# Dividing softmax rows on GpSimd: a per-row scalar operand in place of a repeated column

## The chip, the cores and the metric

The kernel runs on one core of one Trainium2 chip. A core has a matrix engine (TensorE, PE in the profile, with its weight loads as PEld), a vector engine (VectorE, DVE), an activation engine (ScalarE, ACT), a general engine (GpSimd, POOL) and a queue engine (SyncE, SP) that issues most transfers. The metric is device time in microseconds (us). Before the change three runs gave 652.29, 652.94 and 653.63 us, a median of 652.94.

## The reference, cut to what matters

The model is a two-layer encoder trunk over 512 tokens of width 1024, all in fp32. Layer 0 mixes tokens by neighbourhood attention with 16 heads of width 64 (each query sees an 8 x 16 window of a 64-wide grid), layer 1 by dense latent attention with 16 heads (query and key width 96, value width 64). Around both stand RMS norms, a SiLU gate, an output projection and a gated per-layer embedding. What the change touches is the softmax of both attentions:

```python
# layer 0, per grid row of queries
s = jnp.einsum('bwhd,biwjhd->bhwij', q_r, k_win).astype(jnp.float32) * scale
s = (s + bias[None]).reshape(B, H, GRID_W, kr * kc)
pr = jax.nn.softmax(s, axis=-1).reshape(B, H, GRID_W, kr, kc).astype(v.dtype)
return jnp.einsum('bhwij,biwjhd->bwhd', pr, v_win)
...
# layer 1, per block of 128 queries
s = jnp.einsum('bqhd,bkhd->bhqk', qblk, k).astype(jnp.float32) * scale
pr = jax.nn.softmax(s, axis=-1).astype(v.dtype)
return jnp.einsum('bhqk,bkhd->bqhd', pr, v)
```

The softmax is exp(s - max) divided by its sum over the keys; queries lie on partitions, so the sum is one number per partition.

## The kernel before, in words

Matrix products of fp32 data are made of three products each: every operand is split into a high part (`hi`) and a rest (`lo`), and high x high, high x rest and rest x high are added up in PSUM. For weights the split is an ACT copy (L100) and a subtraction that runs mostly on POOL (L101); for activations it is `split` (L109 to L114), an ACT copy from PSUM (L110) and a DVE subtraction (L112).

**Neighbourhood attention** is `na_heads` (L406), with eight pairs of heads, and `na_head` (L536) for one head. A head is worked in two halves of two query tiles. For a half, PE writes scores to a bank `ps_S` (L558, L559); DVE adds the bias and takes the row maximum, writing to the tile `ex` (L565, L568); ACT makes the exponentials in place and their row sums `sm` (L576); DVE takes reciprocals `rc` (L578); POOL multiplies each query tile of `ex` by its column of `rc` (L582, 128 x 128 for the first query tile and 128 x 256 for the other three). Then PE transposes `ex` block by block (L594, L596) into banks `ps_T`, ACT and DVE split these into `ph` and `pl`, and PE multiplies with the values into `ps_O` (L608). The tile `ex` has two buffers: DVE can write the scores of a head only once the transposes of the head two before it are done. The projections of the next pair (L123, `ps_mm`), the gate `z` and the output projection are PE's other work there.

**Latent attention** is `mla_heads` (L942) with 64 turns of `score` (L1041), one for each head and block of 128 queries: three matmuls into `ps_S`, a row maximum on DVE (L1052), exponentials and sums on ACT (L1054), a reciprocal on DVE (L1055), and POOL's multiplication of the whole 128 x 512 tile (L1056). `turn` (L1058) transposes the tile three turns later (L155) and splits it; `output` (L1066) multiplies with the values (L1071). `ex` has four buffers here. Pieces of projection for the next heads are laid between by a table (`pieces`, L1082).

**What sets the order.** Each engine runs its instructions in the order in which they stand in its queue. In most of the program a scheduler lays that order down when the kernel is built: it plays the program through with durations that it assumes for each operation, and puts an instruction where, by these, its operands are there. Where the code says `issue_after`, an instruction stands behind a named one. In latent attention the loop at L1152 ties PE's work, turn by turn, to the last matmul before it, so PE's order is mostly the code's there; in neighbourhood attention it is the scheduler's.

Of the kernel before, what the change touches and what calls it, by code (L numbers as in the profile page):

```python
# [16 lines left out]
ALU = mybir.AluOpType  # L17
AX = mybir.AxisListType
PSUM = bass.MemoryType.PSUM
P = 128  # L20
S = 512
# [13 lines left out]
def win(t, r0, r1, off, dims):  # L35

    b = t[r0:r1]
    return bass.AP(tensor=b.tensor, offset=b.offset + off, ap=[list(b.ap[0])] + [list(d) for d in dims])
# [18 lines left out]
class Trunk:  # L57
# [478 lines left out]
    def na_head(self, pool, h, sq, s0, dk, kl, vh):  # L536

        nc = self.nc
        bias = pool.tile([P, 384], F32, name="bias", tag="bias", bufs=3)
        self.last_bias = nc.sync.dma_start(bias, self.a["na_bias"][h])  # L540
        ex = pool.tile([P, 896], F32, name="ex", tag="ex", bufs=2)
        mx = self.small.tile([P, 4], F32, name="mx", tag="mx")
        sm = self.small.tile([P, 4], F32, name="sm", tag="sm")
        rc = self.small.tile([P, 4], F32, name="rc", tag="rc")
        ecol = lambda qt: slice(0, 128) if qt == 0 else slice(256 * qt - 128, 256 * qt + 128)
        for half in range(2):
            sp = self.psum("S")
            for i in range(2):
                qt = 2 * half + i
                o = sp[:, i * 256:(i + 1) * 256]  # L550
                if qt == 0:
                    o = o.rearrange("p (a b) -> p a b", a=2)
                    lq = s0
                    K = lambda t: win(t, 0, P, 0, [[384, 2], [1, P]])
                else:
                    lq = sq[:, qt * P - 64:qt * P + 64]
                    K = lambda t: t[:, (qt - 1) * P:(qt + 1) * P]
                nc.tensor.matmul(o, lq, K(dk), start=True, stop=False)  # L558
                nc.tensor.matmul(o, lq, K(kl), start=False, stop=True)  # L559
            for i in range(2):  # L560
                qt = 2 * half + i
                c = slice(qt, qt + 1)
                if qt == 0:
                    for r, sc in ((slice(0, 64), slice(0, 128)), (slice(64, 128), slice(128, 256))):
                        nc.vector.tensor_tensor_reduce(out=ex[r, 0:P], in0=sp[r, sc], in1=bias[r, 0:P], scale=-1.0,  # L565
                                                       scalar=-NEG, op0=ALU.add, op1=ALU.min, accum_out=mx[r, c])
                else:
                    nc.vector.tensor_tensor_reduce(out=ex[:, ecol(qt)], in0=sp[:, i * 256:(i + 1) * 256],  # L568
                                                   in1=bias[:, P:], scale=-1.0, scalar=-NEG, op0=ALU.add, op1=ALU.min,
                                                   accum_out=mx[:, c])  # L570
            hs = slice(2 * half, 2 * half + 2)
            for i in range(2):
                qt = 2 * half + i
                e = ex[:, ecol(qt)]
                with self.tc.issue_after(self.hold):
                    self.last_exp = nc.scalar.activation(e, e, AF.Exp, scale=-1.0, bias=mx[:, qt:qt + 1],  # L576
                                                         accum_out=sm[:, qt:qt + 1])
            nc.vector.reciprocal(rc[:, hs], sm[:, hs])  # L578
            for i in range(2):
                qt = 2 * half + i  # L580
                e = ex[:, ecol(qt)]
                self.last_norm = nc.gpsimd.tensor_tensor(out=e, in0=e, in1=rc[:, qt:qt + 1].to_broadcast([P, e.shape[1]]),  # L582
                                                         op=ALU.mult)


        pts = []
        E = lambda qt, s: ex[:, 256 * qt - 128 + s * P:256 * qt + s * P]
        apart = lambda t, w, d: win(t, 0, P, 0, [[d, 2], [1, w]])
        for blocks in ([(None, ex[:, 0:P]), (64, E(1, 0)), (320, E(3, 1))],
                       [(0, E(1, 1)), (128, E(2, 0)), (256, E(2, 1)), (384, E(3, 0))]):  # L590
            t = self.psum("T")
            for c, b in blocks:
                if c is None:
                    nc.tensor.transpose(apart(t, 64, 448), b, self.ident)  # L594
                else:
                    nc.tensor.transpose(t[:, c:c + P], b, self.ident)  # L596
            ph = pool.tile([P, S], F32R, name="ph", tag="pt", bufs=8)
            pl = pool.tile([P, S], F32R, name="pl", tag="pt", bufs=8)
            if len(blocks) == 3:
                self.split(apart(ph, 192, 320), apart(pl, 192, 320), apart(t, 192, 320))  # L600
            else:
                self.split(ph, pl, t)
            pts.append((ph, pl))
        O = self.psum("O")
        n = 0
        for kt, o, w, g, c in ((0, 0, 192, 0, 0), (3, 320, 192, 0, 320), (1, 64, 256, 1, 0), (2, 192, 256, 1, 256)):
            for s in pts[g]:
                nc.tensor.matmul(O[:, o:o + w], vh[kt], s[:, c:c + w], start=n == 0, stop=n == 7,  # L608
                                 skip_group_check=True)
                n += 1  # L610
        return O
# [330 lines left out]
    def mla_heads(self, pool, xT, cT, sets, oT):  # L942


        nc, a = self.nc, self.a
# [95 lines left out]
        def score(i):  # L1041
            h, qt = i // 4, i % 4
            st = sets[h // 2 % 2]
            q, k, kk = ((st["qe"], st["ke"], 96), (st["qo"], st["ko"], 128))[h % 2]
            if qt == 0:
                ST[h] = [self.small.tile([P, 4], F32, name=n, tag=n) for n in ("mx", "sm", "rc")]
            mx, sm, rc = (t[:, qt:qt + 1] for t in ST[h])
            sp = self.psum("S")
            Q = lambda s: q[s][0:kk, qt * P:(qt + 1) * P]
            K = lambda s: k[s][0:kk, :]  # L1050
            self.mms(sp, [(Q(0), K(0)), (Q(0), K(1)), (Q(1), K(0))])
            nc.vector.reduce_max(mx, sp, axis=AX.X, negate=True)  # L1052
            ex = EX[i] = pool.tile([P, S], F32, name="ex", tag="ex", bufs=4)
            nc.scalar.activation(ex, sp, AF.Exp, bias=mx, accum_out=sm)  # L1054
            nc.vector.reciprocal(rc, sm)  # L1055
            nc.gpsimd.tensor_tensor(out=ex, in0=ex, in1=rc.to_broadcast([P, S]), op=ALU.mult)  # L1056

        def turn(i):  # L1058
            h, qt = i // 4, i % 4
# [92 lines left out]
        for i in range(70):  # L1152
            work = []
            if i < 64:
                work.append(lambda: score(i))
                work += pieces(i // 8)[i % 8]
            elif i < 68:
                work.append(ple)
            if 3 <= i < 67:
                work.append(lambda: turn(i - 3))  # L1160
            if i >= 8 and i % 4 < 2:
                work.append(lambda: output(i // 4 - 2, i % 4))
            for f in work:
                with self.tc.issue_after(self.last_mm.ins):
                    f()
            if i == 53:
                last = self.last_mm
# [307 lines left out]
```

## Time and profile before

The profiled execution took 653.56 us; its span, from the first to the last instruction, is 651.5 us, so 2.06 us lie around the span. The execution lies 0.62 us above the median of the three runs.

| | busy, us | share of the span |
|---|---|---|
| PE | 640.2 | 98% |
| PEld | 541.9 | 83% |
| ACT | 453.4 | 70% |
| DVE | 427.7 | 66% |
| POOL | 408.4 | 63% |

The neighbourhood attention runs from about 105 to 235 us, the latent attention from about 400 to 556 us. The mean granted PE clock is 0.995 of full speed. PE's matmuls overlap at their ends, so a row's duration is longer than the step from one matmul to the next; the step is read from the starts. An idle time in brackets behind a row is that of the engine just before it, with the work that ended it.

### The profile page before, as it was taken

How to read it: one execution, taken by the hardware profiler on the slowest of the kernel's cores; microseconds unless marked ns; L12 is line 12 of the kernel's file. 1: busy time of each engine (PE TensorE's matmuls, PEld its weight loads, DVE VectorE, ACT ScalarE, POOL GpSimd, SP SyncE). 2: the span in 40 equal slices, each digit the busy share in tenths (PEclk: the TensorE clock that was granted, in tenths of full speed). 3: DMA queues.
4: the chain of work that ended last, by engine and by line, in shares of the span. 5: the costliest groups of instructions: out<-in, count | busy, mean ns of one | idle time of the engine just before them, and what ended most of it. 6: DMA issues, size and time to landing. Idle time of an engine off the chain costs nothing.

```text
span 651.5 us, 9980 instructions
## 1 busy us (share of the span) xinstructions
PE 640.2 (98%) x3299; PEld 541.9 (83%) x3299; DVE 427.7 (66%) x886; ACT 453.4 (70%) x903; POOL 408.4 (63%) x371
## 2 busy tenths in 40 slices
PE   9999999999999999999999999999999999999994
PEld 6888878888888888888999887888888888888884
DVE  6197987565665616569715514898988885474665
ACT  7575766887886733788644535897989897547855
POOL 0471006877978853797655516786969887437974
PEclk9999999999999999999999999999999999999997
DMA  9939725778958989446643245120112223683524
GB/s 326 355 124 306 217 66 179 263 205 217 229 209 217 239 178 342 147 154 188 224 140 102 78 109 156 32 75 24 49 50 66 65 84 112 229 292 126 193 65 162
DMA packets 46131, 107.41 MB, mean 165 GB/s; under 512 B 4736, under 2 KB 17792, under 8 KB 46080
## 3 DMA queue, kind: packets, MB, share of 16 engines
q1 hardware_dynamic: 34608, 87.12, 39.3%
q0 software_dynamic: 11040, 18.88, 13.6%
q10 hardware_dynamic: 432, 0.79, 0.3%
q8 instruction: 26, 0.43, 0.3%
q14 instruction: 25, 0.20, 0.1%
HBM read 95.23 MB, written 25.17 MB: 185 GB/s over the span
## 4 chain that ended last, share of the span: by engine, by line
PE 83%; POOL 1%; ACT 1%; DVE 0%; DMA 0%; issue 0%; POOLq 0%
PE ps_mm L123 27%; PE ps_S L123 10%; PE ps_mm L959 7%; PE ps_T L155 6%; PE ps_T L851 5%; PE ps_O L1071 5%; PE ps_mm L851 3%; PE ps_S L851 3%; PE ps_O L608 2%; PE ps_T L123 2%; PE ps_O L123 2%; PE ps_mm L909 2%; PE ps_T L301 2%; PE ps_T L596 2%; PE ps_S L909 1%; PE ps_S L559 1%
## 5 line engine op out<-in xcount | busy, mean ns | idle before, releaser
L101 POOL TENSOR_TENSOR wwlo<-wraw,wwhi 128x1024 fp32r<-128x1024 f32 (+5 forms) x68 | 122.3, 1810 | 93.5 <-ACT wwhi L100 41.9
L796 POOL TENSOR_TENSOR wlo<-wraw,whi 128x512 fp32r<-128x512 f32 x56 | 72.7, 1331 | 22.3 <-ACT whi L794 20.2
L1056 POOL TENSOR_TENSOR ex<-ex,rc 128x512 f32<-128x512 f32 x64 | 66.2, 1043 | 26.6 <-DVE rc L1055 22.5
L100 ACT ACTIVATE wwhi<-wraw 128x1024 fp32r<-128x1024 f32 (+5 forms) x71 | 55.1, 799 | 34.3 <-PE ps_mm L123 18.9
L1054 ACT ACTIVATE ex<-ps_S,mx 128x512 f32<-128x512 f32 x64 | 44.0, 687 | 12.6 <-DVE mx L1052 10.9
L1052 DVE TENSOR_REDUCE mx<-ps_S 128x1 f32<-128x512 f32 x64 | 43.7, 683 | 8.4 <-PE ps_S L123 7.7
L582 POOL TENSOR_TENSOR ex<-ex,rc 128x128 f32<-128x128 f32 (+1 forms) x64 | 37.5, 701 | 17.7 <-DVE rc L578 17.5
L112 DVE TENSOR_TENSOR pt_lo<-ps_T,pt_hi 128x512 fp32r<-128x512 f32 x64 | 43.1, 680 | 7.1 <-ACT pt_hi L110 6.7
L110 ACT ACTIVATE pt_hi<-ps_T 128x512 fp32r<-128x512 f32 x64 | 37.7, 594 | 3.4 <-PE ps_T L155 3.0
L155 PE MATMUL ps_T<-ident,ex 128*128 128x128 f32 x256 | 38.3, 272 | 0.0
L155 PEld LDWEIGHTS ps_T<-ident,ex 128*128 128x128 f32 x256 | 31.5, 140 | 7.5
L123 PE MATMUL ps_mm<-xh,wwhi 128*128 128x512 f32 x120 | 33.7, 404 | 0.0
L221 DVE TENSOR_TENSOR u<-ps_O,u 64x512 f32<-64x512 f32 x32 | 21.9, 685 | 17.7 <-ACT u L220 17.2
L576 ACT ACTIVATE ex<-ex,mx 128x128 f32<-128x128 f32 (+1 forms) x64 | 30.2, 473 | 4.2 <-DVE mx L565 4.1
L123 PE MATMUL ps_mm<-xl,wwhi 128*128 128x512 f32 x120 | 31.9, 395 | 0.0
L794 ACT ACTIVATE whi<-wraw 128x1024 fp32r<-128x1024 f32 x28 | 29.3, 1057 | 3.2 <-DMA wraw<-sum 2.4
L123 PE MATMUL ps_mm<-xh,wwlo 128*128 128x512 f32 x120 | 31.1, 394 | 0.0
L123 PE MATMUL ps_S<-ke,qe 96*128 96x512 f32 x96 | 28.9, 407 | 0.3 <-DMA qe<-rl 0.3
L123 PE MATMUL ps_S<-ko,qo 128*128 128x512 f32 x96 | 28.9, 409 | 0.0
L959 PE MATMUL ps_mm<-cT,wwhi 128*128 128x512 f32 x94 | 27.7, 393 | 0.0
L220 ACT ACTIVATE u<-ps_O 64x512 f32<-64x512 f32 x32 | 18.9, 591 | 12.0 <-PE ps_O L608 8.8
L225 POOL TENSOR_TENSOR u<-u,z 128x512 f32<-128x512 f32 x16 | 22.6, 1412 | 7.5 <-DVE u L221 7.5
(488 smaller groups left out, 1915.1 us busy)
## 6 DMA issues: line engine op xcount, KB each, us to landing
sum<-gate POOLq DMA_DIRECT2D x12, 1024.0 KB, 8.2
wraw<-na_qk SPq DMA_DIRECT2D x16, 512.0 KB, 4.9
wraw<-sum SPq DMA_DIRECT2D x16, 512.0 KB, 3.3
pe<-pe SPq DMA_DIRECT2D x31, 256.0 KB, 5.9
wraw<-gate SPq DMA_DIRECT2D x12, 512.0 KB, 3.3
wraw<-na_v SPq DMA_DIRECT2D x10, 512.0 KB, 3.4
sum<-sum POOLq DMA_DIRECT2D x4, 1024.0 KB, 11.1
wraw<-na_o SPq DMA_DIRECT2D x8, 512.0 KB, 4.8
```

Of the source, the lines that this page charges most:

```text
L100: nc.scalar.activation(hi[:, c], raw[:, c], AF.Copy)
L101: f = lambda e, c=c: e.tensor_tensor(out=lo[:, c], in0=raw[:, c], in1=hi[:, c].bitcast(F32), op=ALU.subtract)
L110: self.last_copy = self.act.activation(hi, src, AF.Copy, scale=scale)
L112: self.dve.tensor_tensor(out=lo, in0=src, in1=hi.bitcast(F32), op=ALU.subtract)
L123: last = self.last_mm = nc.tensor.matmul(out, l, r, start=i == 0, stop=i == n - 1)
L155: self.last_mm = self.nc.tensor.transpose(t[:, i * P:(i + 1) * P], b, self.ident)
L796: nc.gpsimd.tensor_tensor(out=lo[:, o], in0=raw[:, o], in1=hi[:, o].bitcast(F32), op=ALU.subtract)
L851: mm = nc.tensor.matmul(ps, l, r, start=j == 0 and p in banks, stop=j == 11 and p in (2, 3, 4), skip_group_check=True)
L959: self.last_mm = nc.tensor.matmul(PS[key], *terms[i], start=i == 0, stop=i == len(terms) - 1)
L1052: nc.vector.reduce_max(mx, sp, axis=AX.X, negate=True)
L1054: nc.scalar.activation(ex, sp, AF.Exp, bias=mx, accum_out=sm)
L1056: nc.gpsimd.tensor_tensor(out=ex, in0=ex, in1=rc.to_broadcast([P, S]), op=ALU.mult)
```

## The change

Both divisions keep their place in the program, their engine, their data and their result. Instead of a tensor-by-tensor multiplication, whose second tensor is the column `rc` read again for each element of a row, they become a tensor-by-scalar multiplication, whose scalar is one number per partition, read from the same column. There are 64 of them in neighbourhood attention (16 of 128 x 128 and 48 of 128 x 256) and 64 of 128 x 512 in latent attention.

```diff
@@ na_head
             for i in range(2):
                 qt = 2 * half + i
                 e = ex[:, ecol(qt)]
-                self.last_norm = nc.gpsimd.tensor_tensor(out=e, in0=e, in1=rc[:, qt:qt + 1].to_broadcast([P, e.shape[1]]),
-                                                         op=ALU.mult)
+                self.last_norm = nc.gpsimd.tensor_scalar(e, e, rc[:, qt:qt + 1], None, op0=ALU.mult)
@@ score
             nc.vector.reciprocal(rc, sm)
-            nc.gpsimd.tensor_tensor(out=ex, in0=ex, in1=rc.to_broadcast([P, S]), op=ALU.mult)
+            nc.gpsimd.tensor_scalar(ex, ex, rc, None, op0=ALU.mult)
```

The scheduler takes the new operation into account, and the order changes on all engines from the neighbourhood attention on. The changed kernel is a line shorter, so its lines behind L582 are numbered one lower (L594 becomes L593, L1056 becomes L1055).

**PE, in the middle of neighbourhood attention.** `ps_T_1504` and `ps_T_1512` hold the transposes of head 5 (counted from 0), `ps_O_1463` is the output of head 4, `ps_S_1625` holds scores of head 6 and `ps_S_1683` of head 7. Before:

```order
L594 MATMUL ps_T_1504<-ident_71,ex_1475 128x2x64
L608 MATMUL ps_O_1463<-ph_1450,Q00_679 128x192
L558 MATMUL ps_S_1625<-da_1403,s0_1411 128x256
L608 MATMUL ps_O_1463<-pl_1451,Q00_679 128x192
L608 MATMUL ps_O_1463<-ph_1450,Q10_502 128x192
L608 MATMUL ps_O_1463<-pl_1451,Q10_502 128x192
L608 MATMUL ps_O_1463<-ph_1459,Q00_679 128x256
L608 MATMUL ps_O_1463<-pl_1460,Q00_679 128x256
L608 MATMUL ps_O_1463<-ph_1459,Q10_502 128x256
L608 MATMUL ps_O_1463<-pl_1460,Q10_502 128x256
L596 MATMUL ps_T_1504<-ident_71,ex_1475 128x128 x2
L596 MATMUL ps_T_1512<-ident_71,ex_1475 128x128 x4
```

And now:

```order
L593 MATMUL ps_T_1504<-ident_71,ex_1475 128x2x64
L558 MATMUL ps_S_1683<-db_1404,s0_1413 128x256
L595 MATMUL ps_T_1504<-ident_71,ex_1475 128x128
L595 MATMUL ps_T_1512<-ident_71,ex_1475 128x128
L559 MATMUL ps_S_1683<-lb1_513,s0_1413 128x256
L558 MATMUL ps_S_1683<-db_1404,sb_1367 128x256
L559 MATMUL ps_S_1683<-lb1_513,sb_1367 128x256
L558 MATMUL ps_S_1696<-db_1404,sb_1367 128x256
L595 MATMUL ps_T_1512<-ident_71,ex_1475 128x128 x2
```

The transposes of head 5 stood beside the scores of head 6 and now stand among those of head 7: a head's transposes have moved further behind its scores.

**PE, at the end of neighbourhood attention.** `ps_T_2259` and `ps_T_2267` hold the transposes of head 12, `ps_O_2276` is its output, `ps_mm_2509` a projection for the gate, `ps_S_2355` holds scores of head 14, `ps_S_2413` of head 15, `ps_T_2317` transposes of head 13. Before:

```order
L594 MATMUL ps_T_2259<-ident_71,ex_2230 128x2x64
L596 MATMUL ps_T_2259<-ident_71,ex_2230 128x128
L596 MATMUL ps_T_2267<-ident_71,ex_2230 128x128
L559 MATMUL ps_S_2305<-lb0_509,sb_1979 128x256
L596 MATMUL ps_T_2267<-ident_71,ex_2230 128x128 x2
L123 MATMUL ps_mm_2509<-xh0_158,wwhi_2504 128x512
L123 MATMUL ps_mm_2509<-xh1_159,wwhi_2504 128x512 x2
L596 MATMUL ps_T_2259<-ident_71,ex_2230 128x128
L596 MATMUL ps_T_2267<-ident_71,ex_2230 128x128
L123 MATMUL ps_mm_2509<-xh1_159,wwhi_2504 128x512 x2
L123 MATMUL ps_mm_2509<-xl0_160,wwhi_2504 128x512 x4
L558 MATMUL ps_S_2355<-da_2216,s0_2224 128x256
```

And now:

```order
L593 MATMUL ps_T_2259<-ident_71,ex_2230 128x2x64
L595 MATMUL ps_T_2259<-ident_71,ex_2230 128x128
L595 MATMUL ps_T_2267<-ident_71,ex_2230 128x128 x3
L595 MATMUL ps_T_2259<-ident_71,ex_2230 128x128
L595 MATMUL ps_T_2267<-ident_71,ex_2230 128x128
L607 MATMUL ps_O_2276<-ph_2263,Q01_680 128x192
L558 MATMUL ps_S_2413<-db_2217,s0_2226 128x256
L559 MATMUL ps_S_2413<-lb1_513,s0_2226 128x256
L558 MATMUL ps_S_2413<-db_2217,sb_2180 128x256
L559 MATMUL ps_S_2413<-lb1_513,sb_2180 128x256
L593 MATMUL ps_T_2317<-ident_71,ex_2288 128x2x64
```

The projection `ps_mm_2509`, which stood between the transposes and what needs them, has moved ahead of this place; the output of head 12 now follows its own transposes with one transpose between.

**POOL, in latent attention.** `wwlo` are weight rests, `rl` a rotary key or query part, `u` and `o1l` belong to the gated output. Before:

```order
L101 TENSOR_TENSOR wwlo<-wraw,wwhi 128x512 x2
L995 TENSOR_TENSOR rl<-rl,rope_s 128x512
L1056 TENSOR_TENSOR ex<-ex,rc 128x512
L996 TENSOR_TENSOR rl<-rh,rl 128x512
L1056 TENSOR_TENSOR ex<-ex,rc 128x512 x2
L998 TENSOR_TENSOR rl<-rl,rh 128x512
L101 TENSOR_TENSOR wwlo<-wraw,wwhi 128x192 x2
L1056 TENSOR_TENSOR ex<-ex,rc 128x512 x3
L225 TENSOR_TENSOR u<-u,z 128x512
```

And now:

```order
L101 TENSOR_TENSOR wwlo<-wraw,wwhi 128x512 x2
L994 TENSOR_TENSOR rl<-rl,rope_s 128x512
L1055 TENSOR_SCALAR ex<-ex,rc 128x512 x3
L995 TENSOR_TENSOR rl<-rh,rl 128x512
L1055 TENSOR_SCALAR ex<-ex,rc 128x512 x2
L997 TENSOR_TENSOR rl<-rl,rh 128x512
L101 TENSOR_TENSOR wwlo<-wraw,wwhi 128x192 x2
L225 TENSOR_TENSOR u<-u,z 128x512
L1055 TENSOR_SCALAR ex<-ex,rc 128x512 x3
```

Two divisions have moved ahead of the rotary sum; PE's order beside them is the same there.

## The prediction

> **What bounds the kernel now.** I read the shares of busy time first, then the chain that ended last, then what PE waited for.
>
> ```profile
> span 651.5 us, 9980 instructions
> PE 640.2 (98%) x3299; PEld 541.9 (83%) x3299; DVE 427.7 (66%) x886; ACT 453.4 (70%) x903; POOL 408.4 (63%) x371
> PE 83%; POOL 1%; ACT 1%; DVE 0%; DMA 0%; issue 0%; POOLq 0%
> PE ps_T L301 <- ACT s L51: 1.2, 1, 1.2
> PE ps_T L596 <- POOL ex L582: 0.3, 1, 0.3
> ```
>
> PE is busy for 98% of the span, the chain is PE's to 83% and POOL's to 1%, and in all PE waited for a division once, for 0.3 us. Ends of matmuls are modelled, so I looked whether their starts hide stalls:
>
> ```profile
> 148.44 1.98 PE L123 MATMUL ps_mm<-xl,wwhi 128*128 128x512 f32 x8
> 150.25 1.98 PE L123 MATMUL ps_mm<-xh,wwlo 128*128 128x512 f32 x8
> 152.07 0.27 PE L594 MATMUL ps_T<-ident,ex 128*128 128x128 f32 x1
> ```
>
> Eight matmuls of 512 columns take 1.81 and 1.82 us from start to start, 0.227 us each; PE keeps that step through both attentions. POOL's place in the two stages that the change touches is read from stretches within them and from POOL's groups there:
>
> ```profile
> core 0: us, PE busy (x) PEld busy (x) DVE busy (x) ACT busy (x) POOL busy (x), PEclk, DMA share, GB/s
> 118.00:222.00 104.00, 103.67 (x611) 90.76 (x610) 66.62 (x226) 83.85 (x209) 83.91 (x88) 1.00 0.85 224
> 400.00:550.00 150.00, 149.70 (x822) 125.84 (x821) 122.95 (x248) 128.41 (x283) 119.99 (x113) 1.00 0.22 67
> L582 POOL TENSOR_TENSOR ex<-ex,rc 128x256 f32<-128x256 f32 x39 | 26.4, 789 | 1.5 <-DVE rc L578 1.5
> L582 POOL TENSOR_TENSOR ex<-ex,rc 128x128 f32<-128x128 f32 x13 | 7.3, 564 | 14.6 <-DVE rc L578 14.6
> L1056 POOL TENSOR_TENSOR ex<-ex,rc 128x512 f32<-128x512 f32 x64 | 66.2, 1043 | 26.6 <-DVE rc L1055 22.5 <-PE ps_S L123 2.4 <-PE ps_O L1071 1.6
> ```
>
> PE is full in both. POOL has 104.00 - 83.91 = 20.1 us free in the first stretch (13 heads) and 150.00 - 119.99 = 30.0 us in the second (64 divisions). It is not the bound, but it isn't far from it either: 80% busy in both.
>
> **What the new operation costs.** No row shows a POOL operation on a wide tile with one tensor and a scalar read per partition. The nearest rows:
>
> ```profile
> L101 POOL TENSOR_TENSOR wwlo<-wraw,wwhi 128x512 fp32r<-128x512 f32 x13 | 16.6, 1294 | 1.2 <-ACT wwhi L100 1.2
> L512 POOL MEMSET la<- 64x512 f32 x2 | 1.0, 522 | 0.1
> L1308 POOL TENSOR_SCALAR rowa<-mn 128x1 f32<-128x1 f32 x4 | 0.9, 225 | 0.0
> L582 POOL TENSOR_TENSOR ex<-ex,rc x64: 391/613/1595, 111.1 to 225.7; 128x256 f32<-128x256 f32 x48, 128x128 f32<-128x128 f32 x16
> 131.80 1.19 POOL L582 TENSOR_TENSOR ex<-ex,rc 128x256 f32<-128x256 f32 x2
> ```
>
> Two tensors of 512 columns take 1.294 us, one tensor and a repeated column 1.043, no source at all (MEMSET) 0.522. The step from a real second tensor to a repeated one is worth 0.25 us, so dropping the second stream may be worth as much again: I take 0.8 us for 512 columns, between 0.522 (nothing read) and 1.043 (today's price), and keep 1.294 as the upper bound of the likeliest case, since the instruction still has to fetch its scalar. By columns: the fastest division in neighbourhood attention takes 0.391 us for 128 columns, the quiet ones of 256 take 1.19 / 2 = 0.595; that is 1.6 ns a column and some 0.19 us fixed, and 0.19 + 512 x 1.6 ns = 1.0 fits the row of 512.
>
> [...]
>
> **What of it reaches the end.** At 0.8 us POOL gains 64 x 0.24 = 15 us in latent attention and perhaps 10 in the other. All of it lies beside PE. How far ahead of PE the divisions are today shows at one tile of latent attention:
>
> ```profile
> 446.28 0.95 PE L123 MATMUL ps_S<-ko,qo 128*128 128x512 f32 x3
> 454.86 0.60 PE L155 MATMUL ps_T<-ident,ex 128*128 128x128 f32 x4
> L1052 DVE TENSOR_REDUCE mx<-ps_S 128x1 f32<-128x512 f32 x64 | 43.7, 683 | 8.4 <-PE ps_S L123 7.7
> L1054 ACT ACTIVATE ex<-ps_S,mx 128x512 f32<-128x512 f32 x64 | 44.0, 687 | 12.6 <-DVE mx L1052 10.9
> ```
>
> Scores that start at 446.28 are transposed three turns later, at 454.86. Between the end of the scores (447.2) and that start lie 7.6 us, and the maximum, exponentials and division need 0.68 + 0.69 + 1.04 = 2.4 plus a reciprocal and queueing. PE's order there is the code's and hardly changes. Term: 0. If that cover were gone, each 0.1 us too many per division would cost 6.4 us.
>
> In neighbourhood attention the order of PE does change. Counted over the order with PE's measured steps (0.227 us for 512 columns, 0.12 for 256, 0.11 for a transpose), a head's first transpose stood 5.8 to 10.7 us behind the last score of its first half (head 1 to 15); now it is 11 to 19.5 us for heads 1 to 12, and 5.1, 7.5 and 12.3 us for heads 13, 14 and 15. So through the middle there is more room than before, whatever the division costs up to a point. Two places at the end give terms:
>
> ```profile
> 220.79 0.33 PE L608 MATMUL ps_O<-ph,Q 128*128 128x192 f32 x1
> 221.45 0.33 PE L596 MATMUL ps_T<-ident,ex 128*128 128x128 f32 x1 [0.33 <-POOL ex L582]
> 221.88 0.49 ACT L110 ACTIVATE ph<-ps_T 128x384 fp32r<-128x384 f32 x1 [1.02 <-PE ps_T L596]
> 218.30 3.10 POOL L582 TENSOR_TENSOR ex<-ex,rc 128x128 f32<-128x128 f32 x4 [1.75 <-DVE rc L578]
> ```
>
> - *Removed.* At 220.79 PE takes 0.66 us to its next start, some 0.12 of it its own: it waits 0.54 us for head 14, whose four divisions took 3.10 us. There the order now has 7.5 us, and the divisions are shorter: -0.54 us.
> - *Added.* Output of head 12 now stands right behind its transposes. A transpose that starts at 221.45 is split at 221.88 + 0.49 = 222.37, so 0.92 us pass before the output can start; the new order leaves two transposes, 0.22 us: +0.70 us. For head 11 it leaves 0.69 us: +0.23 us. What queues behind on PE are scores of head 15 and transposes of head 13, and nothing behind those is due sooner. If the scheduler's other moves hide this, it is 0; if the packed heads 12 to 14 wait for each other through the two `ex` buffers, up to 3 us.
>
> The transfers are the same in number and size; on SP some bias and weight loads swap places, and PE's only stall on a transfer there is 0.3 us, outside this stage. Term: 0. **Sum:** -0.54 + 0.70 + 0.23 = +0.4 us on 653.56, the profiled execution's own time: 653.96. That execution lies 0.62 above the median of the runs, so against the runs 653.3 us.
>
> **The rivals.** *First: POOL becomes the bound (slower).* The operation has two arithmetic slots, of which the change fills one; if POOL runs it as a general two-step loop, the price per column could be double today's. POOL fills up in latent attention when each division takes 30.0 / 64 = 0.47 us more, at 1.51 us, and in neighbourhood attention when a head's four take 20.1 / 13 = 1.55 us more. With doubled columns, 512 cost 1.043 + 0.85 = 1.90 us: 64 x 0.85 = 54.7, less the 30.0 free, makes +24.7 us. A head costs 3 x 0.41 + 0.21 = 1.44 us more, which is just inside the free time: some +2 us of badly fitting waits. Time: 653.3 + 26.7 = 680. With everything doubled (2.09 us): 66.8 - 30.0 = +36.8, and per head 2.18 x 13 - 20.1 = +8.2, so about 698. Against it: no one-source row is above 0.25 us, and dropping a real stream made today's operation cheaper. For it: the one-source rows are all of 1 to 4 columns and say nothing of the price per column; and the scheduler, which knows the operation, laid the transposes further behind, as it would for a slower division. That is an assumption of the scheduler and no measurement, but I have no row that contradicts it.
>
> *Second: the last heads of neighbourhood attention are packed too tightly (slower).* With a division below 1.3 us but the waits through `ex` at their 3 us: 656. For it: PE's filler work (`ps_mm_2509`) has moved ahead of them. Against it: `ex` of head 13 is free at head 11's transposes, 3 us before its own are due, which is about what its chain needs.
>
> *Third: it gets faster.* The only stalls of PE that a division ends are the 0.54 us; without the added ones, and with a little gained at the outputs, 652. To be faster by more than 0.2% PE would have to be slowed by something that its steps do not show.
>
> **How the numbers follow.** This kernel's measurement tells about 0.2% (1.3 us) from no change. Likeliest, no measurable change at 653.3: 0.44, its own range 652 to 655. First rival: 0.43. Second: 0.06. Third: 0.07. So faster 0.07, same 0.44, slower 0.49: the single likeliest time is unchanged, but the slower cases together weigh as much. The range has to reach across the first rival up to its full doubling, 698, and down to 651.8.
>
> **What would show it.** In the changed kernel's groups, the mean of L1055 on 128x512: 0.6 to 1.3 us for my forecast, above 1.5 for the first rival. With the forecast, POOL's busy time in the two stages falls and PE keeps 98%; stalls of PE on `ps_O L607` behind ACT or DVE near 210 to 220 us show the added term, and no wait of PE on `ex L582`. With the first rival, POOL's share in the latent stage goes to 95% or more, PE waits for `ex L1055` turn after turn, and the chain of waits runs through POOL. With the second, a gap of PE of 1 to 3 us stands just before the output projection. The forecast is wrong if L1055 is cheap and the time still moves by more than 1.3 us; then the order did it, not the operation.

## The result, and the profile after

The changed kernel takes **669.14 us** (median of 5 runs, 668.70 to 670.87) against 652.94 (652.29 to 653.63) before: ratio 1.0251, 95% interval 1.0236 to 1.0265. It is 16.2 us slower. The profiled execution took 670.87 us, 1.7 above the median. The shares of busy time and the chain that ended last, for the changed kernel:

```profile
span 668.9 us, 9993 instructions
...
PE 647.5 (97%) x3299; PEld 542.7 (81%) x3299; DVE 429.7 (64%) x886; ACT 454.1 (68%) x903; POOL 462.0 (69%) x371
...
PE 73%; POOL 4%; DVE 4%; ACT 3%; issue 1%; DMA 0%; POOLq 0%; SPq 0%; DVEq 0%; ACTq 0%
```

POOL has 53.6 us more work (462.0 - 408.4), not less, and the chain, which was PE's to 83% and is now to 73%, passes through POOL, DVE and ACT for 11%. POOL's divisions in the changed kernel (busy us in total, mean ns of one, then idle time before them):

```profile
L1055 POOL TENSOR_SCALAR ex<-ex,rc 128x512 f32<-128x512 f32 x64 | 99.8, 1571 | 6.2 <-DVE rc L1054 5.6 <-PE ps_S L123 0.4 <-PE ps_T L155 0.2
L582 POOL TENSOR_SCALAR ex<-ex,rc 128x256 f32<-128x256 f32 x48 | 45.5, 1047 | 0.0
L582 POOL TENSOR_SCALAR ex<-ex,rc 128x128 f32<-128x128 f32 x16 | 12.9, 805 | 3.7 <-DVE rc L578 3.7
```

A division of 512 columns takes 1.571 us where it took 1.043. Busy times in three stretches of the changed kernel: the first as the prediction quoted it, the end of neighbourhood attention, and the 150 us from the first latent scores on (the prediction's stretch began 1.1 us ahead of them):

```profile
core 0: us, PE busy (x) PEld busy (x) DVE busy (x) ACT busy (x) POOL busy (x), PEclk, DMA share, GB/s
118.00:222.00 104.00, 101.00 (x582) 87.46 (x581) 62.59 (x212) 80.35 (x200) 95.09 (x83) 1.00 0.80 209
210.00:235.00 25.00, 20.65 (x112) 17.46 (x112) 15.24 (x57) 16.70 (x47) 22.14 (x23) 0.86 0.81 186
408.45:558.45 150.00, 143.34 (x773) 116.77 (x772) 118.61 (x236) 121.86 (x266) 141.64 (x104) 1.00 0.19 59
```

The end of neighbourhood attention before the change:

```profile
210.00:235.00 25.00, 24.67 (x149) 21.57 (x149) 13.67 (x48) 17.39 (x43) 19.52 (x22) 1.00 1.03 208
```

PE, which was full in both attentions, is idle for 4.4 of 25 us at the end of neighbourhood attention and for 6.7 of 150 in latent attention, where POOL is now busy for 94%. The first latent scores start at 408.45 us instead of 401.14, and the last matmul starts at 659.8 instead of 642.5. So **7.3 us are lost up to the end of neighbourhood attention and 10.0 us behind that**, nearly all in latent attention. Together that is 17.3 us, the distance of the two profiled executions (670.87 and 653.56 us); the medians lie 16.2 us apart, and the last section shows what the profiled execution of the changed kernel has of its own. What PE waited for in the whole changed kernel (us, times, longest; the first six lines):

```profile
PE ps_T L155 <- POOL ex L1055: 3.5, 6, 1.0
PE ps_S L558 <- DVE mx L568: 2.0, 2, 1.4
PE ps_S L123 <- ACT ex L1053: 1.6, 3, 0.6
PE ps_S L123 <- DMA qe<-rl: 1.5, 2, 1.0
PE ps_S L123 <- DVE mx L568: 1.4, 1, 1.4
PE ps_O L607 <- DVE u L221: 1.0, 2, 0.7
```

Only the first of these is a wait for a division. The others are waits for ACT, DVE and a transfer, and two kinds of cause offer themselves: the **price** of the new operation, and the **order** into which the scheduler put all engines once the source named another operation. The first experiments part the two.

### The profile page after: what moved, and what is told of

Read it like the earlier page. It is cut to its first block, busy times and chain, and to the rows that moved or that the text cites. A ratio compares the mean times of both kernels' runs of the same rounds, so it can differ in the third digit from the quotient of the medians.

```text
span 668.9 us, 9993 instructions
## 1 busy us (share of the span) xinstructions
PE 647.5 (97%) x3299; PEld 542.7 (81%) x3299; DVE 429.7 (64%) x886; ACT 454.1 (68%) x903; POOL 462.0 (69%) x371
## 4 chain that ended last, share of the span: by engine, by line
PE 73%; POOL 4%; DVE 4%; ACT 3%; issue 1%; DMA 0%; POOLq 0%; SPq 0%; DVEq 0%; ACTq 0%
PE ps_mm L123 26%; PE ps_S L123 8%; PE ps_T L155 5%; PE ps_T L850 5%; PE ps_mm L958 4%; PE ps_mm L850 3%; PE ps_O L1070 3%; PE ps_S L850 3%; PE ps_T L123 2%; PE ps_O L123 2%; PE ps_O L607 2%; PE ps_mm L908 2%; PE ps_T L301 2%; PE ps_T L595 1%; PE ps_S L908 1%
## 5 line engine op out<-in xcount | busy, mean ns | idle before, releaser
L1055 POOL TENSOR_SCALAR ex<-ex,rc 128x512 f32<-128x512 f32 x64 | 99.8, 1571 | 6.2 <-DVE rc L1054 5.6
L582 POOL TENSOR_SCALAR ex<-ex,rc 128x128 f32<-128x128 f32 (+1 forms) x64 | 56.0, 986 | 3.7 <-DVE rc L578 3.7
L123 PE MATMUL ps_mm<-xh,wwlo 128*128 128x512 f32 x120 | 33.4, 400 | 0.0
L123 PE MATMUL ps_mm<-xh,wwhi 128*128 128x512 f32 x120 | 31.5, 397 | 0.0
```

The source lines that it names most:

```text
L123: last = self.last_mm = nc.tensor.matmul(out, l, r, start=i == 0, stop=i == n - 1)
L582: self.last_norm = nc.gpsimd.tensor_scalar(e, e, rc[:, qt:qt + 1], None, op0=ALU.mult)
L1055: nc.gpsimd.tensor_scalar(ex, ex, rc, None, op0=ALU.mult)
```

## The experiments

In most of these kernels the scheduler sets the order of the kernel before, or of the changed one, and only then are the POOL operations that divide `ex` by `rc` exchanged, each with its own waits and signals. Every engine then keeps its order instruction for instruction. The edit is this one, later with another condition or another form of the operation:

```
+                if to_scalar:
+                    b.instructions[k] = mybir.InstTensorScalarPtr(op0=ALU.mult, op1=ALU.bypass, **same)
+                else:
+                    b.instructions[k] = mybir.InstTensorTensor(op=ALU.mult, **same)
...
+    exchange(nc, lambda width, n: True, True)
```

The runs in one table. The last two columns come from each profiled execution: how much later than in the kernel before the first latent scores start (401.14 us there), and how much longer it is from there to the last matmul (241.37 us there). Where nothing changed in a stage these move by up to 0.7 us. The first of them also holds a drop of PE's clock that some of these executions have, up to some 2 us (last section).

| kernel | median us | ratio (95%) | before latent attention | from there on |
|---|---|---|---|---|
| changed kernel | 669.14 | 1.0251 (1.0236 to 1.0265) | +7.3 | +10.0 |
| old order, new operation | 670.41 | 1.0261 (1.0246 to 1.0277) | +7.1 | +9.7 |
| new order, old operation | 669.59 | 1.0261 (1.0241 to 1.0281) | +6.7 | +9.0 |
| new order, divisions of 64 columns | 668.59 | 1.0232 (1.0213 to 1.0250) | +6.7 | +8.8 |
| old order, divisions of 64 columns | 652.55 | 0.9991 (0.9981 to 1.0000) | -0.6 | -0.6 |
| old order, new operation in light groups | 656.99 | 1.0061 (1.0044 to 1.0078) | -0.6 | +4.1 |
| old order, new operation in heavy groups | 657.33 | 1.0064 (1.0049 to 1.0079) | +0.7 | +3.5 |
| old order, new operation on 416 columns | 655.98 | 1.0043 (1.0028 to 1.0058) | -0.1 | +2.4 |
| new order, reciprocals freed | 669.47 | 1.0255 (1.0233 to 1.0276) | +6.9 | +8.9 |
| new order, exponentials freed | 660.35 | 1.0106 (1.0085 to 1.0127) | +6.0 | +2.2 |
| second step used, order left to the scheduler | 653.36 | 1.0009 (1.0000 to 1.0018) | -0.4 | +0.3 |
| second step used, old order | 652.79 | 1.0002 (0.9993 to 1.0011) | -0.6 | -0.6 |

### Price or order

The old order with all 128 operations exchanged:

> Every engine keeps the order of the kernel before; only the 128 divisions on POOL are now tensor-scalar operations with the same waits. Price theory (the operation is 1.5 times dearer, and POOL is full in places): latent attention loses its 9 to 11 us as with the change, neighbourhood attention between 0 and 6 us, since there the old order leaves less room behind the scores; 662 to 670 us in all. Order theory (the scheduler's new order of PE brought the loss): 653 us, or 662 to 664 if only the 7 us of neighbourhood attention are the order's.

It took 670.41 us. The price alone brings the whole loss. What PE waits for with the old order and the new operation:

```profile
PE ps_T L155 <- POOL ex L1056: 7.0, 6, 2.3
PE ps_T L596 <- POOL ex L582: 4.1, 9, 1.4
```

Here PE waits for divisions in both attentions, 15 times, as the first rival of the prediction had it. In neighbourhood attention more than half of the loss, 4.2 of 7.1 us, has come by 205 us, at heads where the old order has transposes close behind the scores.

The other way round, the changed kernel's order with the old operation:

> Every engine keeps the order of the changed kernel; the 128 divisions are the old operation with the repeated column. Price theory: nothing of the loss is left, 652 to 654 us. Order theory: 659 to 669 us, 7 us at least of the loss staying at the end of neighbourhood attention.

It took 669.59 us: **the order alone brings the whole loss too**, with divisions as cheap as before. Neither theory said that each would be enough. What PE waits for in this kernel between 400 and 565 us:

```profile
PE ps_S L123 <- ACT ex L1053: 3.5, 5, 1.0
PE ps_S L123 <- DMA qe<-rl: 1.4, 2, 0.9
PE ps_S L123 <- DVE mx L1051: 1.0, 1, 1.0
PE ps_mm L958 <- DVE vt L112: 0.6, 1, 0.6
```

No wait for a division is left; PE waits mostly for exponentials and maxima to free a bank of scores.

The two causes don't add up: 7.1 and 6.7 make 7.3, 9.7 and 9.0 make 10.0. In latent attention the waits say how they share. With the price alone PE waits 7.0 us for divisions, with the order alone 3.5 for exponentials, with both 3.5 and 1.6. PE, late for one of them, finds the other ready. That is read from the waits; no run shows it by itself.

### Does the order need POOL at all

> Order of the changed kernel on every engine; all 128 divisions are the old operation, cut to 64 columns (the other columns stay undivided), some 0.3 us each. If the new order loses its time without POOL (in the queues of ACT and DVE, where maxima and exponentials now stand behind other work): 665 to 669 us, as with the full old operation. If the place of the divisions in POOL's queue brings it: 660 us or less.

> The same cut to 64 columns in the order of the kernel before: what divisions of almost no cost would be worth there. PE is busy for 98% of the span and waited once for a division, for 0.3 us of 0.5 us of stall: 652.5 to 653.5 us by every theory; below 651 us the divisions hold up PE in a way that its waits don't show.

```
+    exchange(nc, lambda width, n: ("tensor", 64))
```

In the new order 668.59 us, in the old one 652.55. With divisions of 0.3 us (0.293 measured in latent attention) the new order still loses 15.3 us, so the price of the divisions has next to no part in what the order costs. The second run also closes the third rival of the prediction: divisions of next to no cost are worth 0.4 to 0.7 us against the kernel before, which is inside what this kernel's measurement can tell.

### What the order costs in latent attention

The order of PE in latent attention is the same in both kernels, matmul for matmul, up to the last turns. ACT's and DVE's are not. What these two waited for in latent attention, kernel before (401 to 556 us):

```profile
ACT ex L1054 <- DVE mx L1052: 10.9, 16, 1.1
DVE rc L1055 <- ACT ex L1054: 10.7, 21, 1.4
DVE mx L1052 <- PE ps_S L123: 7.7, 17, 2.6
```

and in the changed order with the old operation (408 to 563 us):

```profile
ACT ex L1053 <- DVE mx L1051: 21.9, 31, 1.5
DVE rc L1054 <- ACT ex L1053: 18.6, 34, 1.4
DVE mx L1051 <- PE ps_S L123: 3.7, 5, 2.6
```

Exponentials wait twice as long for maxima, reciprocals nearly twice as long for exponentials, and maxima seldom wait for their scores any more: they are late for another reason, which must be what stands ahead of them in DVE's queue. First suspect were the reciprocals:

> Order of the changed kernel on every engine, all divisions the old operation with the repeated column (that much alone took 669.6 us); in latent attention DVE's 64 reciprocals read a constant table and no longer wait for ACT's sums, and the division on POOL waits for ACT in their place (the divisors are then not the sums: that part of the computation is left out). In the new order 54 of the 64 maxima stand behind the reciprocal of the turn before, where it was 41. If those waits in DVE's queue are what the new order costs in latent attention: its 9 us go, and the 7 us at the end of neighbourhood attention stay, 660 to 662 us. If ACT's or another queue does it: 667 to 670 us.

```
+                if t == "InstReciprocal" and o in wide:
...
+                    b.instructions[k] = mybir.InstReciprocal(
+                        ins=[mx], outs=list(i.outs),
+                        sync_info=mybir.SyncInfo(on_wait=[w for w in si.on_wait if w not in act], on_update=list(si.on_update)),
+                        **again(i))
```

669.47 us: nothing is won, and this suspicion falls. DVE and ACT in that kernel (408 to 563 us):

```profile
DVE pt_lo L112 <- ACT pt_hi L110: 15.7, 16, 2.0
...
ACT ex L1053 <- DVE mx L1051: 17.5, 28, 1.6
```

The reciprocals wait for nothing, but the next instruction in the queue does: `pt_lo`, the split of an earlier turn's transposes, which needs ACT's `pt_hi` (5.5 us of waiting before this edit, 15.7 now). In the new order 51 of the stage's 64 `pt_hi` stand behind the exponential of a turn at least three newer, where it was 37. So DVE waits for ACT's split, ACT's split waits behind an exponential, and that exponential waits for DVE's maximum. Cut at the maximum:

> Order of the changed kernel on every engine, all divisions the old operation; in latent attention the maxima read a constant table, and each exponential waits for its scores alone, with a constant in place of the maximum (that part of the computation is left out). With the reciprocals freed nothing was won (669.5 us): the maxima then stood waiting behind the split of an earlier turn, which waits for ACT. If the new order's loss in latent attention goes through the maxima, which stand behind other work in DVE's queue so that the exponentials free PE's score banks late: its 9 us go, 660 to 662 us. If ACT's queue alone sets when the exponentials run: 666 to 670 us.

```
+                if o.startswith("ex_") and mine(i, "InstActivation"):
...
+                    L[k] = mybir.InstActivation(
+                        func=i.func, ins=[i.ins[0], column, mybir.ImmediateValue(dtype=mybir.dt.float32, value=0.001), i.ins[3]], outs=list(i.outs),
+                        sync_info=mybir.SyncInfo(on_wait=[w for w in si.on_wait if not w.ant_name.startswith("DVE")]
+                                                 + scores[str(i.ins[0].memref)], on_update=list(si.on_update)),
+                        **again(i))
```

660.35 us, as expected: of the 9.0 us in latent attention 2.2 are left, and the loss ahead of it stays. PE's waits for exponentials and maxima are gone there, and 1.3 us of waiting for a transfer (`qe<-rl`) stay. The order's cost in latent attention runs through the exponentials' wait for DVE's maxima. The edit takes out two waits at once, that of the maximum for its scores and that of the exponential for its maximum, and no run parts them. That the two queues hold each other up in turn is how the waits read; which of the moved instructions does most was not tried.

### What the order costs at the end of neighbourhood attention

Here no run takes a link away; what follows is read from the changed kernel's trace. Start and duration, PE and DVE:

```profile
214.34 0.60 PE L595 MATMUL ps_T<-ident,ex 128*128 128x128 f32 x4
...
215.07 0.28 DVE L565 CUSTOM_DVE_ANT_0 ex<-ps_S,bias 64x128 f32<-64x128 f32 x1 [0.39 <-POOL ex L582]
...
216.29 0.35 PE L558 MATMUL ps_S<-da,s 128*128 128x256 f32 x1 [1.35 <-DVE mx L568]
...
224.61 1.05 PE L595 MATMUL ps_T<-ident,ex 128*128 128x128 f32 x4
...
227.01 1.19 PE L123 MATMUL ps_S<-wwhi,oh 128*128 128x512 f32 x2 [1.35 <-DVE mx L568]
...
228.01 1.05 PE L123 MATMUL ps_S<-wwhi,ol 128*128 128x512 f32 x2
```

Scores of one head now stand right behind the transposes of an earlier one. The transposes free a buffer of `ex`; only then can DVE empty a bank of scores into it (215.07), and only then can PE write the next scores (216.29). The row at 215.07 names a division of POOL as what DVE waited for. But DVE's wait for PE's signal ends in the trace at 214.99, just behind the fourth transpose (214.94), and with the old operation, whose divisions end at other times, it again ends 0.05 us behind the fourth transpose. In the middle of the stage other matmuls lie between, and PE is busy for all of the 92 us from 118 to 210 us; at the end there are none. The same happens at 224.61 and 227.01, and with the old operation in this order at the same places. With the median step of each shape between 118 and 205 us of the kernel before as the usual one, PE's time on top of its usual steps between 210 and 235 us adds up to 8.6 us here (idle time and slower steps together), 7.1 with the old operation and 0.8 before.

### How dear is too dear

In the old order, half of latent attention's divisions at a time:

> Order of the kernel before; tensor-scalar only in 32 of latent attention's 64 divisions, in those groups of eight turns (1st, 3rd, 5th, 7th) in which POOL has little other work (10.6 to 13.0 us of 16.6 to 18.4 busy before). Theory of a full POOL in bursts: 32 x 0.52 = 17 us more of POOL's time find room, at most +1 us: 653 to 654 us. Theory of a uniform price (each dearer division delays PE a little, through its own latency): half of the 10 us, 658 us.

> The same with the other 32 divisions, in the groups (2nd, 4th, 6th, 8th) in which POOL was busy for 16.7 to 18.8 us of 19.1 to 19.5 before. Theory of a full POOL in bursts: 8 x 0.52 = 4.2 us a group are added to 2.4, 0.3, 0.5 and 2.6 us of room, so 1.8 + 3.9 + 3.7 + 1.6 = 11 us too much, of which slack of the turns may hide some: +7 to +11, 660 to 664 us. Theory of a uniform price: 658 us, as with the light groups.

```
+    exchange(nc, lambda width, n: width == S and (n - 65) // 8 % 2 == 0, True)
```

(with 1 in place of 0 for the heavy groups). 656.99 and 657.33 us: the forecasts of the bursts miss in both, and the uniform price's 658 is the nearer. The groups with room on average cost as much as those without. But the price isn't uniform either, as the stretches show. Two stretches with the new operation in the light groups:

```profile
440.00:460.00 20.00, 20.00 (x107) 16.55 (x106) 17.04 (x35) 17.42 (x39) 15.72 (x12) 1.00 0.06 20
460.00:480.00 20.00, 18.29 (x108) 15.50 (x107) 15.81 (x32) 15.34 (x35) 19.67 (x19) 1.00 0.27 80
```

and in the heavy ones:

```profile
440.00:460.00 20.00, 20.00 (x106) 16.39 (x105) 17.55 (x38) 16.96 (x38) 14.56 (x14) 1.00 0.07 20
460.00:480.00 20.00, 19.12 (x110) 15.85 (x109) 16.70 (x35) 16.38 (x38) 20.00 (x17) 1.00 0.25 74
```

In both it is the second stretch, a heavy one, in which PE loses time, and so it is again from 500 to 520 us. The light group's dear divisions cost nothing where they run (PE 20.00); they bring POOL later into the burst that follows (19.67 of 20.00 busy), and the burst has no room to catch up in.

An intermediate price, over 416 of the 512 columns:

> Order of the kernel before on every engine; in latent attention the 64 divisions are tensor-scalar operations over 416 of their 512 columns (the last 96 columns of each row stay undivided), by the two prices seen (0.599 us for 128 columns, 1.56 for 512, so 2.5 ns a column) 1.32 us each instead of 1.04; neighbourhood attention as before. Threshold of the prediction (POOL decides from 1.51 us a division on average): 653 us. Carried delay (POOL's bursts have almost no room, so whatever is added to the divisions there and just ahead of them reaches PE): half of what 1.56 us cost in this stage, 0.28 / 0.52 x 9.75 = 5.2, so 657 to 659 us.

655.98 us, at a measured 1.327 us each. Below the carried delay's 657 to 659 and above the threshold's 653, so neither holds as it was put. In latent attention 1.04 us a division costs nothing, 1.33 costs 2.4 us, 1.56 costs 9.7: it begins somewhere below 1.33 and grows steeply, (9.7 - 2.4) / (64 x 0.237) = half a microsecond of time for each microsecond of work.

### Why the operation is dear, and a form that isn't

> Order of the kernel before; in latent attention the operation changes with each sixteen divisions: tensor-scalar as in the change; tensor-scalar with the number 1.0 in place of the reciprocals (division left out); tensor-scalar with a second multiplication by 1.0; a copy (division left out). If reading a scalar per row costs the extra time, the number is near 1.04 us or below and the second multiplication near 1.6. If the general two-step loop costs it, both stay at 1.5 to 1.6 us. If a second step is really run only when it is asked for, the second multiplication takes 2 us or more. The copy, one stream and no arithmetic, 0.5 to 1.0 us.

```
+    exchange(nc, lambda width, n: (["scalar", "number", "two", "copy"][(n - 65) // 16], S) if width == S else (None, 0))
```

The forms in order, each from a stretch of that kernel in which only it ran or from the whole span:

```profile
L1056 POOL TENSOR_SCALAR ex<-ex,rc 128x512 f32<-128x512 f32 x13 | 20.2, 1566 | 1.2 <-DVE rc L1055 1.0
L1056 POOL TENSOR_SCALAR ex<-ex 128x512 f32<-128x512 f32 x16 | 23.6, 1488 | 3.9 <-DVE rc L1055 3.9
L1056 POOL TENSOR_SCALAR ex<-ex,rc 128x512 f32<-128x512 f32 x14 | 9.6, 691 | 8.1 <-DVE rc L1055 7.3 <-PE ps_T L155 0.8
L1056 POOL COPY ex<-ex 128x512 f32<-128x512 f32 x16 | 9.7, 612 | 9.6 <-DVE rc L1055 9.3 <-PE ps_S L123 0.2
```

(The whole of that kernel took 657.71 us, in one run.) None of the three theories holds; only the copy came as expected. Reading the scalar costs 0.08 us (1.566 against 1.488 with a number). And the operation gets **cheaper by 0.875 us when it has more to do**: with a second multiplication by 1.0 it takes 0.691 us, near the bare copy's 0.612. The slow thing here is a tensor-scalar operation whose second step is empty: 1.488 to 1.566 us for 512 columns, against 0.691 with both steps.

So the change was tried again with both steps, in its own order and in the old one:

> The change once more, with the second arithmetic step of each tensor-scalar operation used, a multiplication by 1.0 (0.69 us for 512 columns, where the change's operation took 1.57), the order left to the scheduler, which makes a third one of it: in latent attention 38 of 64 maxima behind the reciprocal of the turn before (41 in the kernel before), elsewhere new. Price and queue theory: no loss in latent attention; at the end of neighbourhood attention 0 to +7, since that order is new too: 652 to 660 us. If any new order costs what the changed kernel's did: 667 us or more.

> The same operation with the used second step, in the order of the kernel before. Divisions of almost no cost gave 652.5 us in this order, the old operation 653.3: 652.4 to 653.2 us by the price theory. Above 655 us would mean that this form hurts something beside POOL.

```
-            nc.gpsimd.tensor_scalar(ex, ex, rc, None, op0=ALU.mult)
+            nc.gpsimd.tensor_scalar(ex, ex, rc, 1.0, op0=ALU.mult, op1=ALU.mult)
```

(and in the same way at the other place). 653.36 and 652.79 us against 652.92: no difference beyond 0.2% in either. The busy times with the order left to the scheduler:

```profile
PE 640.2 (98%) x3299; PEld 542.5 (83%) x3299; DVE 426.7 (66%) x886; ACT 454.1 (70%) x903; POOL 382.4 (59%) x371
```

POOL is relieved by 26.0 us over the span (408.4 to 382.4), and PE, at 98%, gets nothing of it, which is what the prediction had said of a cheaper division. It also shows that a new order is not dear as such: this one, a third, loses nothing.

## Why the prediction was right, and where it failed

The time lies inside the range, and on the side to which the cases together leaned. The likeliest single value, 653.3, missed by 15.8 us. What came is the first rival's mechanism and the second's at once, and beside them a cost of the new order in latent attention that no case had. No case gives 669 us: that the time lies in the range owes much to its width of 46 us, and the agreement with the number is in part luck. The signs named for the first rival came in part: a division of 1.57 us, POOL at 94% of the latent stage, but 6 waits of PE for 64 divisions and not one in turn after turn.

**What bounds the kernel** was right: relieving POOL by 26 us changes nothing, and near-free divisions are worth at most 0.7 us.

**What the new operation costs** is the term that failed first: 0.8 us taken, 1.57 measured, beyond the 1.294 that was kept as the upper bound of the likeliest case. The step from two streams to a repeated column was carried on to one stream, as if streams set the price. They don't: one stream takes from 0.69 to 1.57 us depending on whether the second step is empty. The rival's doubling (1.90) was nearer in size, and its ground, two arithmetic slots of which one is filled, pointed at the right place with the wrong sign: filling the second makes it fast.

**Latent attention, "Term: 0".** It had two reasons. One was that PE's order there is the code's. PE's order was indeed unchanged up to the last turns, but the queues of ACT and DVE were not looked at, and the new order alone cost 9.0 us. The other was the cover of 7.6 us, read at one tile in a light stretch, with the queueing left without a number. At that tile 3.5 us lie between the end of the division and the first transpose; at the head of the first heavy stretch of the kernel before (the first of the two divisions here is the tile's) it is 0.7 us, and at the next one, at 501 us, as little:

```profile
462.55 2.06 POOL L1056 TENSOR_TENSOR ex<-ex,rc 128x512 f32<-128x512 f32 x2
464.26 0.60 PE L155 MATMUL ps_T<-ident,ex 128*128 128x128 f32 x4
```

A division that is 0.53 us dearer, behind others that are dearer too, has no room there.

**The first rival's sum** was right in kind and short in size. (64 x 0.85 is 54.4 and not 54.7, which leaves its 680 us as they are.) By its own working, with the price that was measured, 64 x 0.528 = 33.8 us less the 30.0 free would have left +3.8 in latent attention; the price alone makes +9.7. POOL's free time is not where its work is: it lies in light groups, and whatever delays POOL there meets a burst. The price from which POOL decides, 1.51 us, was therefore too high; at 1.33 something is lost already.

**Neighbourhood attention.** "More room through the middle" was right: there the changed kernel loses nothing, while the old order with the dear operation does. The stall behind head 14's division went, as said. The packed heads were priced at "up to 3 us" and given a chance of 0.06: the mechanism, heads that wait for each other through the two `ex` buffers, is the one that the rows show, and its size was 7 us, since it came three times (1.35, 0.68 and 1.35 us on `mx`; at the second DVE had also been held up by `u`) with waits of the outputs between, and in the profiled execution PE ran at a lower clock behind it (0.50 from 223.30 to 230.00 us, below).

**The chances** treated the price and the order as rivals, one or the other. Each was enough, and together they were no worse than either. That could not be seen in the profile of before; the new order of ACT and DVE could have been.

## What to carry to other kernels

On POOL, time the exact form of an operation at its real width before building on it: fewer sources is no promise (1.57 us for the scalar form on 128x512 here, 1.04 for the repeated column), and here a multiplication by 1.0 that does nothing more than halves the time (1.57 to 0.69 us). Where a scheduler sets the order, an edit of one operation is two changes, its price and a new order of every engine; pin the order and exchange the operation, then do the reverse, before explaining a loss by either. An unchanged order on the bound engine proves little: two helper queues that wait for each other in turn can starve it while each of them is about 80% busy (DVE 118.6 and ACT 121.9 of 150 us here).

## What the runs showed of the hardware

A POOL tensor-scalar operation on 128x512 fp32 takes 1.57 us with one step and 0.69 with two. Why the empty step is slow stays open.

In the profiled execution of the changed kernel PE's granted clock fell behind the stalls at the end of neighbourhood attention. Between 222 and 231 us, and within the drop alone:

```profile
222.00:231.00 9.00, 7.65 (x33) 6.43 (x32) 5.02 (x21) 6.78 (x20) 8.38 (x11) 0.62 0.90 204
223.30:230.00 6.70, 5.35 (x19) 4.40 (x18) 3.72 (x18) 4.55 (x12) 6.08 (x8) 0.50 0.89 230
```

The trace has the clock at half speed from 223.24 to 230.06 us. A matmul of 512 columns took 0.427 us from start to start there instead of 0.227, and the slower steps came to 2.5 us. The drop belongs to this execution more than to the kernel: in the other four the mean granted clock was 0.996 or 0.997 instead of 0.991, and they took 1.6 to 2.2 us less. So a part of the 7.3 us of the first column of the table, some 2 us, is not in the median. The profiled executions of the two kernels that part price and order hold such a drop as well, each of 3.41 us, with slower steps of some 1.7 us (old order, new operation, from 227.30 us) and 1.8 us (new order, old operation, from 218.37 us).

In 3.41 us, the length of the two shorter drops, ahead of each of the three PE was busy for 1.99, 1.76 and 1.83 us. Not each stall brings a drop: in the old order with the new operation PE waited for 2.3 us up to 474.8 us, and the granted clock in the stretch around it was 1.00. What sets it off was not tried.
